# Two queue positions at a kernel's start, and where GpSimd's staging loads may stand

## The chip, the cores and the metric

The kernel runs on one core of one Trainium2 chip. The metric is the device time of one execution in microseconds. Smaller is better. A core has five engines that run their own queues of instructions in order: TensorE (PE in the profile, with its weight loads as PEld), VectorE (DVE), ScalarE (ACT), GpSimd (POOL) and SyncE (SP, which here only issues transfers). GpSimd and ScalarE can issue transfers too.

## The reference, cut to what matters

An encoder layer on two batches (prompt and sample, 1024 rows of 1024 channels each): RMS norm, one wide input projection, a Fourier branch, a Hyena branch with two long convolutions per channel block, gates, and an output projection. The Hyena filters come from a small network with two sine layers.

```python
xn = rmsnorm(x, g_pre)
p = xn @ w_in                                     # 8 sections of 1024 columns
fz = fft(fv, axes=(sequence, channel in group)).real
y_f = (fz * silu(fg)) @ w_fourier_out
h = sin(f1 * (z @ w1 + b1)); h = sin(f2 * (h @ w2 + b2)); h = h @ w3   # filters, then windowed
z = v
for n, gate in enumerate((x1, x2)):
    z = gate * long_conv(z, kf[:, n], hyena_d[n])
y_h = (z * silu(hg)) @ w_hyena_out
out = (g_f * y_f + g_h * y_h) @ w_out
return x + rmsnorm(out, g_post)
```

## The kernel before, in words

Three phases follow each other: `phase_fourier`, `phase_main`, `phase_blocks`. All matrices are split into a rounded high part and a rest (`split`, lines 168 to 174: ScalarE casts the high part, VectorE or GpSimd subtracts), so that a product is three matmuls (`mm3`).

**The start** (batch 0 in `phase_fourier`). `hidden(0)` computes the first sine layer of the filter network: two matmuls, then on VectorE the range reduction of `sin_of` (lines 255 to 270) for two halves, then a Sin on ScalarE for each half (line 270), then a store to DRAM on SP (line 299). `norm` (line 302) loads eight blocks of 128 rows, squares each on ScalarE with the sum beside it (line 319), and for every four blocks computes on VectorE the inverse root (`rstd`, 11 short dependent steps) and scales four identity blocks with it (`dg`, line 324). Those diagonal blocks are the right-hand sides of the transposing matmuls `tpx` in `xtile` (line 342), whose results ScalarE copies out as `xg` (line 343). From `xg` VectorE makes even and odd parts `eo`, split into `eh` and `el`. `weights` (line 359) loads a block `wfv` of the first weights into one of two buffers, adds and subtracts its halves on VectorE (`wer`, `wor`), casts on ScalarE (`we`, `wo`) and subtracts on VectorE. Six projections (`pfv`) run along with the eight column blocks k. The tables `seq` and `chan` are loaded by GpSimd after a one-column copy from `rs` (lines 528 to 532), so not before the inverse roots are there.

**Staging** (`staging`, lines 911 to 934). In the sample batch of `branches`, each convolution step draws twice from a generator of 25 steps. A piece (of 24: three operands q, four k, two halves) is two loads into a buffer `draw` on GpSimd's queue (line 926), eight subtractions and additions of 128x256 on GpSimd (`fold`), and a store to `d_t` (line 932), for the last operand a second store to `d_wo` (line 930). There are two `draw` buffers. The operands are read in `phase_blocks`. Operand 1 is made of `d_g[0][0]`, which the filter stage of `phase_main` writes, operand 2 of `d_sh[0]`, which the prompt batch's convolutions write, and operand 5 of `w_out`. GpSimd also subtracts the low parts `wl` of the input projection's weights (`inproj`, line 716) up to the end of the prompt batch, and multiplies its gates.

**What sets the order.** The Tile framework schedules each engine's queue ahead of time from its own timing of the whole program. `tc.issue_after(ins)` makes the instructions that a block creates on the engine of `ins` follow `ins` in that engine's queue; instructions on other engines get no edge. `self.spectrum` (line 799) is a load that SP issues, and the block at line 923 creates loads on GpSimd.

Of the kernel before, what the change touches and what calls it, by code (L numbers as in the profile page):

```python
# [161 lines left out]
class K:  # L162
# [92 lines left out]
    def sin_of(self, y, k, out, src_ps, f, b):  # L255

        nc = self.nc
        nc.vector.tensor_scalar(y, src_ps, b, f, op0=ADD, op1=MUL)
        magic = 12582912.0
        nc.vector.tensor_scalar(k, y, 1.0 / (2 * math.pi), magic, op0=MUL, op1=ADD)  # L260
        nc.vector.tensor_scalar(k, k, -magic, None, op0=ADD)
        c1 = 6.28125
        r = 2 * math.pi - c1
        c2 = float(_round12(np.array([r]))[0])
        c3 = r - c2
        for c in (c1, c2, c3):
            self.stt("dve", y, k, -c, y)
        pi = 3.1415925
        nc.vector.tensor_scalar(y, y, pi, -pi, op0=ALU.min, op1=ALU.max)
        nc.scalar.activation(out, y, AF.Sin)  # L270

    def hidden(self, layer, px, pf):

        nc, a = self.nc, self.a
        h = px.tile([P, L], F32, tag="eo", name=f"hd_{layer}", bufs=2)
        out = [h[:, 0:512], h[:, 512:1024]]
        z = px.tile([P, L], F32, tag="x", name="hd_z", bufs=3)
        if layer == 0:
            w = pf.tile([P, P], F32, tag="sst", name="hd_w", bufs=1)
            self.hfb = px.tile([P, 4], F32, name="hd_fb", bufs=1)  # L280
            nc.sync.dma_start(z[0:33], a["c_z"])
            nc.scalar.dma_start(w[0:33], a["filt_w1"])
            nc.scalar.dma_start(self.hfb, a["filt_fb"])
            w, z = w[0:33], z[0:33]
            y, k = [[pf.tile([P, 512], F32, tag=f"{t}p{n}", name=f"s{t}", bufs=1 + (t == "p")) for n in range(2)]
                    for t in "qp"]
        else:
            nc.sync.dma_start(z[64:128], self.d_h1[64:128])
            w = px.tile([P, P], F32, tag="xg", name="hd_w", bufs=2)
            nc.sync.dma_start(w[64:128], a["filt_w2"])  # L290
            w, z = w[64:128], z[64:128]
            y, k = [px.tile([P, L], F32, tag="x", name="s" + t, bufs=3) for t in "yk"]
            y, k = [[t[:, 0:512], t[:, 512:1024]] for t in (y, k)]
        for n in range(2):
            p = self.psum("mm", 4, "phd")
            nc.tensor.matmul(p, w, z[:, 512 * n:512 * n + 512], start=True, stop=True)
            self.sin_of(y[n], k[n], out[n], p, self.hfb[:, 2 * layer:2 * layer + 1],
                        self.hfb[:, 2 * layer + 1:2 * layer + 2])
        nc.sync.dma_start(self.d_h if layer else self.d_h1, h)


    def norm(self, b, px, pf):

        nc, a = self.nc, self.a
        ss = px.tile([P, 8], F32, tag="ss", name=f"ss{b}")
        self.rs = rs = px.tile([P, 8], F32, tag="rs", name=f"rs{b}")
        self.diag = dg = px.tile([P, 8, P], F32, tag="dg", name=f"dg{b}", bufs=1)
        self.xs = []  # L310
        for m in range(8):
            if b == 0 and m < 6:
                x = pf.tile([P, D], F32, tag=("fA", "fB", "ee0", "ee1", "oo0", "oo1")[m], name=f"x0_{m}", bufs=1)
            else:
                x = px.tile([P, D], F32, tag="x", name=f"x{b}_{m}", bufs=3)
            nc.sync.dma_start(x, a[f"x{b}"][m * P:(m + 1) * P, :])
            self.xs.append(x)
            sq = px.tile([P, D], F32, tag="xg", name="sq", bufs=2)
            nc.scalar.activation(sq, x, AF.Square, accum_out=ss[:, m:m + 1])
            if m % 4 == 3:  # L320
                q = slice(m - 3, m + 1)
                self.rstd(px, rs[:, q], ss[:, q], 4)
                for j in range(m - 3, m + 1):
                    nc.vector.tensor_scalar(dg[:, j], self.ident, rs[:, j:j + 1], None, op0=MUL)

    def xtile(self, b, k, px, fo):

# [157 lines left out]
    def phase_fourier(self):  # L485
        tc, nc, a = self.tc, self.nc, self.a
        with ExitStack() as es:
            px = es.enter_context(tc.tile_pool(name="px", bufs=1, reuse_waits="tile"))
            pw = es.enter_context(tc.tile_pool(name="fw", bufs=1, reuse_waits="tile"))
            pe = es.enter_context(tc.tile_pool(name="fe", bufs=1, reuse_waits="tile"))  # L490
            pc = es.enter_context(tc.tile_pool(name="fc", bufs=1, reuse_waits="tile"))
            pf = es.enter_context(tc.tile_pool(name="ff", bufs=1, reuse_waits="tile"))
            fo = {}
            fo["x5"] = pc.tile([P, 8, 36], F32R, name="x5")
            fo["x5t"] = pc.tile([P, 260], F32R, name="x5t")
            fo["xx"] = pc.tile([P, 34], F32R, name="xx")
            fo["px"] = pc.tile([P, 514], F32R, name="px")
            fo["ex"] = [pc.tile([P, 4, 34], F32R, name=f"ex{i}") for i in range(2)]
            fo["seq"] = pc.tile([P, 2, 8 * 258], F32R, name="seq")
            fo["alt"] = pc.tile([P, 2 * 86], F32R, name="alt")  # L500
            fo["chan"] = pc.tile([P, 2, 3 * P], F32R, name="chan")
            fo["chx"] = pc.tile([P, 2, 2, P], F32R, name="chx")
            for t in [fo[n] for n in ("x5", "x5t", "xx", "px")] + fo["ex"]:
                if len(t.shape) > 2:
                    t = t.rearrange("p a b -> p (a b)")
                nc.vector.tensor_scalar(t, self.ident[:, 0:1].to_broadcast(list(t.shape)), 0.0, None, op0=MUL)
            for b in range(NB):
                fo["eh"] = pe.tile([P, 8, 2, 2, 256], F32R, tag="eh", name="eh")
                fo["el"] = pe.tile([P, 8, 2, 2, 256], F32R, tag="el", name="el")
                if b == 0:  # L510
                    self.hidden(0, px, pf)
                with tc.issue_after(behind.ins) if b else ExitStack():
                    self.norm(b, px, pf)
                begun = {}
                if b == 0:
                    W = self.open_weights(pw)
                    for e, m in [(0, 0), (0, 1), (0, 2), (0, 3), (1, 0), (1, 1)]:
                        begun[e, m] = self.psum("X", 2, "pfv1") if e else self.psum("mm", 4, "pfv0")
                for k in range(8):
                    if b == 0:  # L520
                        self.weights(pw, W, 0, k, True)
                    self.xtile(b, k, px, fo)
                    for (e, m), p in begun.items():
                        self.pfv(p, e, m, k, W, fo)
                for half in ((0, 1), (1, 0))[b]:
                    if b + half == 0:
                        nc.sync.dma_start(self.vec, a["c_vec"])
                        for t in ("seq", "chan"):
                            nc.gpsimd.tensor_copy(fo[t][:, 0, 0:1], self.rs[:, 7:8])
                        nc.gpsimd.dma_start(fo["seq"], a["c_seq"])  # L530
                        nc.gpsimd.dma_start(fo["alt"], a["c_alt"])
                        nc.gpsimd.dma_start(fo["chan"], a["c_chan"])
                        nc.gpsimd.dma_start(fo["chx"].rearrange("p a b c -> p (a b c)"), a["c_chx"])
                    elif b + half != 2:
                        W = self.open_weights(pw)
                        for k in range(8):
                            self.weights(pw, W, half, k, False)
                        behind = self.rounded
                    self.fourier_half(b, half, W, fo, px, pf, begun)
                    begun = {}  # L540
                    if (b, half) == (1, 1):
                        self.hidden(1, px, pf)


    def butterfly(self, ws, xp, xm):
# [170 lines left out]
    def inproj(self, sec, mt, b=None):  # L716
# [3 lines left out]
        for q in range(2):  # L720
# [8 lines left out]
            else:  # L729
                r = self.wp.tile([P, 512], F32, tag="w", name="wr", bufs=2)  # L730
                nc.sync.dma_start(r, a["w_in"][sec, mt][:, s])
                self.split(*parts, r, "pool", "act")
                if kept:
                    for t, k in zip(parts, kept):
                        nc.gpsimd.dma_start(k[:, s], t.bitcast(F32))
# [175 lines left out]
    def staging(self):  # L911
# [3 lines left out]
        for q, k, half in [(q, k, h) for q in (1, 2, 5) for k in range(4) for h in range(2)] + [(0, 0, 0)]:  # L915
            r = None
            if q:
# [2 lines left out]
                    r = self.stage2.tile([P, 4, 256], F32, tag="draw2", name="draw", bufs=1)  # L920
                else:
                    r = self.cp.tile([P, 4, 256], F32, tag="draw", name="draw", bufs=1)
                with self.tc.issue_after(self.spectrum.ins):
                    for i in range(2):
                        src = {1: self.d_g[0][0], 2: self.d_sh[0]}[q][k + 4 * i] if q < 5 else a["w_out"][(k + 4 * i) * P:(k + 4 * i + 1) * P]
                        nc.gpsimd.dma_start(r[:, 2 * i:2 * i + 2], src.rearrange("p (n c) -> p n c", n=2)[:, :, s])
# [548 lines left out]
```

## Time and profile before

| | us |
|---|---|
| median of 3 runs (2438.82 to 2448.58) | 2444.28 |
| the profiled execution, its own time | 2439.01 |
| its span, first to last instruction | 2437.2 |
| TensorE busy in the span | 2366.3 |
| VectorE, ScalarE, GpSimd busy | 2034.0, 1126.2, 563.5 |
| TensorE busy of the first 40 us | 18.80 |
| TensorE busy of 400 to 800 us | 380.12 |
| TensorE busy of 1200 to 1500 us | 298.51 |

The profile is one execution. A row of its timeline gives start, duration, engine, source line, operation, output and inputs; a bracket at the end gives the idle time before the row and what ended it. A row of the list of waits gives who waited for whom, the total in us, how often, and the longest. A row of groups gives the busy time, the mean duration in ns, and the idle time before. SPq and POOLq are the transfer issues and queue events of those engines.

### The profile page before, as it was taken

The page shows a single profiled execution, that of the slowest core. Times are in us where ns is not written, and L with a number is a line of the kernel's source. Part 1 is how long each engine was busy: PE and PEld are TensorE (multiplying, and loading weights), DVE is VectorE, ACT ScalarE, POOL GpSimd, SP SyncE. Part 2 cuts the span into 40 slices and gives each one's busy share as a digit, 9 for nine tenths or more (in the row PEclk, how much of TensorE's full clock was granted, in tenths as well). Part 3 has the DMA queues.
Part 4 walks back from the last instruction along what each step waited for, and adds up shares of the span by engine and source line. Part 5 has one row for each costly group of instructions (what it writes and reads, how often), then busy time and mean ns, then how long its engine had stood idle before and what let it go on. Part 6 is the DMA issues. An engine that isn't in the chain of part 4 may idle for free.

```text
span 2437.2 us, 37123 instructions
## 1 busy us (share of the span) xinstructions
PE 2366.3 (97%) x13006; PEld 2053.1 (84%) x13006; DVE 2034.0 (83%) x3816; ACT 1126.2 (46%) x2088; POOL 563.5 (23%) x568
## 2 busy tenths in 40 slices
PE   6999999999999999999999999999999999999998
PEld 5988888887878888888888888888878888888786
DVE  7687788788888999999999999997667687778777
ACT  5545666665554333333332222333334365656543
POOL 1341322233343343434334400111200000101000
PEclk9999999999999999999999999999999999999999
DMA  7535644466566455555667644343646687978744
GB/s 272 181 133 203 226 158 156 160 190 186 189 202 211 152 182 177 168 161 174 223 199 265 209 143 137 130 153 128 213 143 219 214 304 249 279 263 227 227 156 155
DMA packets 246850, 470.26 MB, mean 193 GB/s; under 512 B 24758, under 2 KB 88471, under 8 KB 246280
## 3 DMA queue, kind: packets, MB, share of 16 engines
q1 hardware_dynamic: 220076, 380.53, 47.7%
q0 software_dynamic: 26400, 87.35, 10.8%
q8 instruction: 102, 1.67, 0.3%
q14 instruction: 84, 0.69, 0.1%
q10 hardware_dynamic: 188, 0.02, 0.0%
HBM read 300.04 MB, written 167.77 MB: 192 GB/s over the span
## 4 chain that ended last, share of the span: by engine, by line
PE 50%; DMA 1%; DVE 1%; issue 0%; ACT 0%; SPq 0%; DVEq 0%; ACTq 0%
PE pg L194 25%; PE pin L194 16%; PE pT L194 4%; PE pX L194 4%; DMA wh<-d_w 1%; PE tph L787 1%; DMA bl<-d_t 0%; DMA wraw<-d_m 0%; DVE bl L181 0%; DVE wraw L181 0%; DVE gt L181 0%; DVE o L181 0%; DVE o L177 0%; ACT bh L1034 0%; ACT pg L1142 0%
## 5 line engine op out<-in xcount | busy, mean ns | idle before, releaser
L194 PE MATMUL pin<-xh,wh 128*128 128x512 f32 x1472 | 577.9, 394 | 6.4 <-ACT wh L171 1.9
L194 PE MATMUL pin<-xh,wl 128*128 128x512 f32 x1472 | 576.9, 393 | 2.1 <-POOL wl L181 2.1
L194 PE MATMUL pin<-xl,wh 128*128 128x512 f32 x1472 | 578.2, 393 | 0.0
L181 POOL TENSOR_TENSOR wl<-wr,wh 128x512 fp32r<-128x512 f32 x136 | 243.5, 1790 | 885.0 <-ACT wh L171 657.4
L194 PEld LDWEIGHTS pin<-xh,wh 128*128 128x128 f32 x1472 | 277.9, 189 | 58.2 <-DMA wh<-d_w 2.7
L194 PEld LDWEIGHTS pin<-xh,wl 128*128 128x128 f32 x1472 | 278.4, 189 | 53.5 <-POOL wl L181 2.9
L194 PEld LDWEIGHTS pin<-xl,wh 128*128 128x128 f32 x1472 | 278.2, 189 | 50.9
L194 PE MATMUL pT<-cinv,yh 128*128 128x256 f32 x1024 | 192.2, 282 | 0.0
L194 PEld LDWEIGHTS pT<-cinv,yh 128*128 128x128 f32 x1024 | 165.1, 190 | 9.7
L181 DVE TENSOR_TENSOR t<-pX,k 128x1024 f32<-128x1024 f32 x128 | 155.4, 1214 | 8.7 <-PE pX L194 6.6
L194 PE MATMUL pX<-bh,cfwd 128*128 128x256 f32 x768 | 160.7, 287 | 0.2 <-ACT bh L171 0.2
L171 ACT CAST wh<-wr 128x512 fp32r<-128x512 f32 x136 | 83.8, 616 | 150.9 <-PE pin L194 107.0
L171 ACT CAST yh<-y 128x512 fp32r<-128x512 f32 x128 | 79.4, 621 | 160.3 <-DVE y L181 133.4
L194 PE MATMUL pT<-cinv,yl 128*128 128x256 f32 x512 | 144.9, 283 | 1.1 <-DVE yl L181 1.1
L171 ACT CAST bh<-b 128x512 fp32r<-128x512 f32 x144 | 88.7, 619 | 111.4 <-DVE b L181 71.8
L181 DVE TENSOR_TENSOR bl<-b,bh 128x512 fp32r<-128x512 f32 x144 | 115.1, 801 | 19.1 <-ACT bh L171 18.9
L194 PEld LDWEIGHTS pX<-bh,cfwd 128*128 128x128 f32 x768 | 125.7, 191 | 3.6 <-ACT bh L171 0.6
L194 PE MATMUL pX<-bl,cfwd 128*128 128x256 f32 x384 | 109.5, 285 | 0.0
L1231 POOL DMA_DIRECT2D d_m<-gt x32 | 27.5, 860 | 320.2 <-DVE gt L181 288.4
L194 PEld LDWEIGHTS pT<-cinv,yl 128*128 128x128 f32 x512 | 97.7, 191 | 3.5 <-DVE yl L181 1.6
L181 DVE TENSOR_TENSOR yl<-y,yh 128x512 fp32r<-128x512 f32 x128 | 94.2, 736 | 6.5 <-ACT yh L171 6.4
L181 DVE TENSOR_TENSOR y<-t 128x512 f32<-128x512 f32 x128 | 97.6, 763 | 0.8
(354 smaller groups left out, 5718.6 us busy)
## 6 DMA issues: line engine op xcount, KB each, us to landing
k<-d_k SPq DMA_DIRECT2D x128, 512.0 KB, 4.3
wr<-in_w_in SPq DMA_DIRECT2D x136, 256.0 KB, 3.2
d_g<-gt SPq DMA_DIRECT2D x92, 256.0 KB, 2.6
d_k<-kt SPq DMA_DIRECT2D x128, 128.0 KB, 2.2
d_k<-kt SPq DMA_DIRECT2D x64, 256.0 KB, 2.6
fz<-d_g SPq DMA_DIRECT2D x64, 256.0 KB, 5.2
d_t<-draw POOLq DMA_DIRECT2D x24, 512.0 KB, 5.1
d_w<-wh POOLq DMA_DIRECT2D x48, 256.0 KB, 4.0
```

The costliest lines, as they stand in the source:

```text
L171: self.rounded = nc.scalar.copy(h, src)
L181: return e.tensor_tensor(out, a, b, op=op)
L194: return self.nc.tensor.matmul(out, lhsT, rhs, start=start, stop=stop, skip_group_check=shared)
L787: nc.tensor.transpose(tp[:, q * P:(q + 1) * P], eo[:, e, q], self.ident)
L1231: at(t + 0.3, lambda: nc.gpsimd.dma_start(d_m[:, c], box[0], accum_op=ADD))
```

## The change

Three edits. First, `sin_of` no longer issues the Sin; `hidden` returns a function that does so and stores the result, and for the first layer it is called after `norm`, inside `issue_after` the last square. Second, the first weights' blocks are traced inside `issue_after` the last of the eight diagonal scalings, which acts on what `weights` does on VectorE. Third, the staging loads are held behind `self.pooled`, the last subtraction that `inproj` put on GpSimd, instead of `self.spectrum`.

```diff
@@ sin_of
         nc.vector.tensor_scalar(y, y, pi, -pi, op0=ALU.min, op1=ALU.max)
-        nc.scalar.activation(out, y, AF.Sin)
@@ hidden
-        nc.sync.dma_start(self.d_h if layer else self.d_h1, h)
+
+        def sines():
+            for n in range(2):
+                nc.scalar.activation(out[n], y[n], AF.Sin)
+            nc.sync.dma_start(self.d_h if layer else self.d_h1, h)
+        return sines
@@ norm
-            nc.scalar.activation(sq, x, AF.Square, accum_out=ss[:, m:m + 1])
+            self.squared = nc.scalar.activation(sq, x, AF.Square, accum_out=ss[:, m:m + 1])
...
-                    nc.vector.tensor_scalar(dg[:, j], self.ident, rs[:, j:j + 1], None, op0=MUL)
+                    self.scaled = nc.vector.tensor_scalar(dg[:, j], self.ident, rs[:, j:j + 1], None, op0=MUL)
@@ phase_fourier
                 if b == 0:
-                    self.hidden(0, px, pf)
+                    sines = self.hidden(0, px, pf)
                 with tc.issue_after(behind.ins) if b else ExitStack():
                     self.norm(b, px, pf)
+                if b == 0:
+                    with tc.issue_after(self.squared.ins):
+                        sines()
...
                     if b == 0:
-                        self.weights(pw, W, 0, k, True)
+                        with tc.issue_after(self.scaled.ins):
+                            self.weights(pw, W, 0, k, True)
...
-                        self.hidden(1, px, pf)
+                        self.hidden(1, px, pf)()
@@ inproj
                 self.split(*parts, r, "pool", "act")
+                self.pooled = self.left
@@ staging
-                with self.tc.issue_after(self.spectrum.ins):
+                with self.tc.issue_after(self.pooled.ins):
```

ScalarE's queue at the start before the change, from the fifth block's square to the first `xg` copy (`sq` is the output of a square and also the tile that a Sin reads):

```order
L319 ACTIVATE sq,ss_328<-x_4_364 128x1024
L270 ACT_TABLE_LOAD
L270 ACTIVATE hd_296<-sq 128x512
L319 ACTIVATE sq,ss_328<-x_5_368 128x1024
L270 ACTIVATE hd_296<-sq 128x512
L319 ACTIVATE sq,ss_328<-x_6_372 128x1024
L319 ACTIVATE sq,ss_328<-x_7_376 128x1024
L343 ACTIVATE xg_0_417<-tpx,gpre 128x512
```

The same stretch of ScalarE's queue with the change:

```order
L323 ACTIVATE sq,ss_325<-x_4_361 128x1024
L323 ACTIVATE sq,ss_325<-x_5_365 128x1024
L323 ACTIVATE sq,ss_325<-x_6_369 128x1024
L323 ACTIVATE sq,ss_325<-x_7_373 128x1024
L301 ACT_TABLE_LOAD
L301 ACTIVATE hd_296<-sq 128x512 x2
L347 ACTIVATE xg_0_417<-tpx,gpre 128x512
```

The table load and both Sins moved from between the squares to between the last square and the first copy.

VectorE's queue before, from the first four diagonal blocks into the second inverse root (`rs_m`, `rs_329`, `rs_t` are that root's steps):

```order
L324 TENSOR_SCALAR dg_330<-ident,rs_329 128x128 x4
L181 TENSOR_TENSOR wer<-wfv 128x260
L181 TENSOR_TENSOR wor<-wfv 128x256
L241 TENSOR_SCALAR rs_m<-ss_328 128x4
L181 TENSOR_TENSOR wer<-wfv 128x260
L181 TENSOR_TENSOR wor<-wfv 128x256
L242 TENSOR_SCALAR rs_329<-rs_m 128x4
L181 TENSOR_TENSOR we_398<-wer,we_397 128x260
L250 SCALAR_TENSOR_TENSOR rs_t<-rs_329 128x4
L181 TENSOR_TENSOR wo_400<-wor,wo_399 128x256
```

VectorE's queue with the change, from the last step of the second inverse root:

```order
L252 SCALAR_TENSOR_TENSOR rs_326<-rs_t,rs_326 128x4
L328 TENSOR_SCALAR dg_327<-ident,rs_326 128x128 x4
L181 TENSOR_TENSOR wer<-wfv 128x260
L181 TENSOR_TENSOR wor<-wfv 128x256
L181 TENSOR_TENSOR wer<-wfv 128x260
L181 TENSOR_TENSOR wor<-wfv 128x256
L181 TENSOR_TENSOR we_398<-wer,we_397 128x260
L181 TENSOR_TENSOR wo_400<-wor,wo_399 128x256
```

The eight operations on the weights of k = 0 and 1, which stood between the steps of the second root, now stand behind its diagonal blocks. On ScalarE the casts of the weights of k = 2 now stand ahead of the copies `xg_2` and those of k = 3 behind them; before, ahead of `xg_2` stood the casts of k = 4 and 5.

GpSimd's queue before, around the second piece of operand 1 (`d_g_0_1` and `d_g_0_5` are written in the filter stage):

```order
L926 DMA draw<-d_g_0_1_126 128x2x256 x2
L181 TENSOR_TENSOR wl<-wr,wh 128x512 x6
L926 DMA draw<-d_g_0_5_130 128x2x256 x2
L181 TENSOR_TENSOR wl<-wr,wh 128x512
L181 TENSOR_TENSOR draw<-draw 128x256 x8
L932 DMA d_t_241<-draw 128x4x256 x2
```

GpSimd's queue with the change, where the first pieces of operand 1 now stand, at the end of the prompt batch:

```order
L744 DMA d_w_7_1_236<-wl 128x512
L181 TENSOR_TENSOR wl<-wr,wh 128x512 x2
L935 DMA draw<-d_g_0_0_125 128x2x256
L935 DMA draw<-d_g_0_4_129 128x2x256
L935 DMA draw<-d_g_0_0_125 128x2x256
L935 DMA draw<-d_g_0_4_129 128x2x256
L181 TENSOR_TENSOR draw<-draw 128x256 x7
L941 DMA d_t_241<-draw 128x4x256
```

All 24 pieces now stand behind the last `wl` of the prompt batch; before, the eight of operand 1 stood in the filter stage and the first of operand 2 in the prompt batch's convolutions. On TensorE and VectorE the queues of the convolution stage hold the same instructions in another interleaving.

## Prediction

> **What bounds the kernel now.** First the page, for the busy shares, then the list of TensorE's waits, then stretches, then the timeline of the stretches in which TensorE idles.
>
> ```profile
> PE 2366.3 (97%) x13006; PEld 2053.1 (84%) x13006; DVE 2034.0 (83%) x3816; ACT 1126.2 (46%) x2088; POOL 563.5 (23%) x568
> PE tpx L194 <- DVE dg L324: 14.5, 2, 8.9
> 0.00:40.00 40.00, 18.80 (x94) 15.43 (x95) 27.35 (x86) 22.71 (x40) 4.38 (x17) 0.98 0.85 290
> 40.00:60.00 20.00, 20.00 (x166) 20.00 (x166) 18.04 (x40) 13.54 (x20) 3.52 (x6) 0.95 0.68 232
> 400.00:800.00 400.00, 380.12 (x2030) 325.40 (x2030) 336.06 (x735) 230.69 (x492) 139.90 (x134) 0.98 0.58 188
> ```
>
> TensorE bounds the kernel: of 2437.2 us of span it idles 70.9. Of these, 21.2 lie in the first 40 us, where the transposes wait 14.5 for the diagonals, and 19.9 in the 400 us that hold the filter stage. From 40 us on TensorE is full, so time that the start gains is kept. The change can only win out of these two patches and a few waits near 1130 us, and can only lose where TensorE is now full.
>
> **Edits 1 and 2, the start: the last square.** In the timeline of the start:
>
> ```profile
> 13.02 0.33 SPq L886 DMA_DIRECT2D th<-in_c_th  x1
> 13.08 1.06 ACT L319 ACTIVATE sq<-x 128x1024 f32<-128x1024 f32 x1 [0.67 <-DMA x<-in_x]
> 14.25 1.28 ACT L270 ACT_TABLE_LOAD   x1
> 14.28 0.33 SPq L886 DMA_DIRECT2D wsh<-in_w_short  x1
> 15.54 0.63 ACT L270 ACTIVATE hd<-sq 128x512 f32<-128x512 f32 x1
> 15.55 0.33 SPq L886 DMA_DIRECT2D bm<-in_b_merge  x1
> 16.08 1.04 ACT L319 ACTIVATE sq<-x 128x1024 f32<-128x1024 f32 x1
> 18.68 1.04 ACT L319 ACTIVATE sq<-x 128x1024 f32<-128x1024 f32 x1
> 19.84 0.17 DVE L241 TENSOR_SCALAR rs_m<-ss 128x4 f32<-128x4 f32 x1 [1.56 <-ACT sq L319]
> ```
>
> Table load and two Sins (1.28 + 2 x 0.63 = 2.5 us) stand before the last three squares. Without them the squares wait for their rows. SP's small issues are released one per landed block of x: the fifth square starts at 13.08, next to the issue at 13.02, so the sixth and seventh blocks landed near 14.3 and 15.6, and I take 16.9 for the eighth by the same spacing. The last square then runs from 16.9 to 17.95 instead of to 19.72: 1.8 us.
>
> **The second root and its diagonals.**
>
> ```profile
> 22.41 0.16 DVE L250 SCALAR_TENSOR_TENSOR rs_t<-rs 128x4 f32<-128x4 f32 x1
> 23.59 0.88 DVE L324 TENSOR_SCALAR dg<-ident,rs 128x128 f32<-128x128 f32 x4
> 23.93 7.04 PE L194 MATMUL tpx<-dg,x 128*128 128x128 f32 x40 [5.59 <-DVE dg L324]
> ```
>
> From the first step at 19.84 to the diagonals at 23.59 it takes 3.75 us, because eight operations on weights stand in between. The last six steps, free of them, take 23.59 - 22.41 = 1.18, 0.20 each, so 11 take 2.2: 1.55 us less. The diagonals come 1.8 + 1.55 = 3.3 us earlier, near 20.3.
>
> **What is late next.** The table load and two Sins (2.5 us) now stand between the last square (18.1 with its accumulator read) and the first xg copy, which comes at 20.7; TensorE needs the bank that this copy frees from about 21.0, so this costs some 0.4 us. The eight weight operations follow the diagonals (0.35 apart, 2.8 us, from 21.2) and are covered by the transposes (7.04). The real price is in the loads: a buffer of wfv is free only when its sums are done.
>
> ```profile
> 24.10 0.53 POOL L530 DMA_DIRECT2D seq<-in_c_seq  x1 [0.18 <-POOL chan L529]
> L363 SPq DMA_DIRECT2D wfv<-in_w_fv x2: 328/328/328, 18.3 to 20.7; - x2
> DMA to landing us min/median/max: 2.9/3.1/3.3
> ...
> L363 SPq DMA_DIRECT2D wfv<-in_w_fv x1: 328/328/328, 25.2 to 25.2; - x1
> DMA to landing us min/median/max: 10.2/10.2/10.2
> 35.41 0.43 DVE L181 TENSOR_TENSOR wer<-wfv 128x260 f32<-128x260 f32 x1 [1.78 <-DMA wfv<-in_w_fv]
> 37.96 1.27 ACT L343 ACTIVATE xg<-tpx,gpre 128x512 f32<-128x512 f32 x2
> 38.70 4.57 PE L194 MATMUL tpx<-dg,x 128*128 128x128 f32 x24 [3.10 <-ACT xg L343]
> ```
>
> The two weight blocks issued at 18.3 and 20.7 are those of k = 2 and 3; they land in about 3.1 us. The one issued at 25.2, of k = 4, is caught behind seq on the shared DMA engines: 10.2 us, until 35.4. ScalarE has the casts of k = 4 and 5 ahead of xg_2, so TensorE's transposes of k = 3 wait until 38.70. With the change seq is issued near 20.9, and now k = 2 and 3 are caught behind it: issued near 22.1 and 22.8 (sums done; the store of the sine layer, which SP issues ahead of them, is ready at 20.7), landing near 22.1 + 10.2 + 1 = 33.3 (the store's bytes share the engines) and 34.3. But only k = 2 stands ahead of xg_2, so the copies run at about 34.3 and the transposes at 35.0: 38.70 - 35.0 = 3.7 us. Bounds: a landing after 3.1 us would leave the limit to the 3.3 us of the diagonals plus up to 2.2 of the chain behind, 5.5; a landing at 35.5 leaves 1.5. k = 4 and 5 are issued after that without seq and land in about 3.1 us, before the projections ask. **First term: -3.7.**
>
> A rule of the Trainium skill ("ScalarE: Activation LUTs", What ACT_TABLE_LOAD costs) puts a drain of 1.38 us behind each table load of 1.28. The row at 14.25 ends at 15.53 and the Sin starts at 15.54, so the trace shows the load and no drain. By the page the first copy would come 1.4 us later and the term would be about -2.3, an estimate.
>
> **Edit 3, what leaves the prompt batch.** The old block named an instruction of SP, and the loads are GpSimd's, so they were not held and GpSimd waited for them with other work behind.
>
> ```profile
> L181 POOL TENSOR_TENSOR draw<-draw x32: 717/741/1190, 487.1 to 681.0; 128x256 f32<-128x256 f32 x32
> 545.54 1.44 POOL L926 DMA_DIRECT2D draw<-d_g  x2 [6.84 <-DMA d_g<-gt]
> 546.27 2.58 DVE L181 TENSOR_TENSOR bl<-b,bh 128x512 fp32r<-128x512 f32 x1
> L181 DVE TENSOR_TENSOR bl<-b,bh 128x512 fp32r<-128x512 f32 x10 | 6.8, 683 | 2.5 <-ACT bh L171 2.5
> 548.91 0.39 PE L194 MATMUL pXf<-bl,cfwd 128*128 128x256 f32 x1 [1.00 <-DVE bl L181]
> 558.84 0.36 PE L194 MATMUL pXf<-bh,cfwd 128*128 128x256 f32 x1 [2.09 <-DVE kt L177]
> 682.45 0.36 PE L194 MATMUL pXf<-bh,cfwd 128*128 128x256 f32 x1 [1.08 <-ACT dec L621]
> 1132.95 0.50 PE L194 MATMUL pin<-xh,wl 128*128 128x512 f32 x1 [1.27 <-POOL wl L181]
> 1137.31 0.71 PE L194 MATMUL pX<-b,cfw 128*128 128x128 f32 x4 [1.12 <-DVE b L181]
> ```
>
> The first row is operand 1's folds in the filter stage. At 546 VectorE's bl (0.68 in a stretch without staging, the group row) lasts 2.58 beside GpSimd's late issues and the wl behind them; TensorE waits 1.00 and then 2.09. After the last fold of 681 it waits 1.08, and near 1133 1.27 and 1.12, where the first piece of operand 2 stands ahead of a wl. Together 6.6 us stand close behind a piece. Upper bound: all the idle time of that stretch, (681 - 487)/400 x 19.9 = 9.7, and the last two waits, 12.0 in all. Lower bound: 0, if the next wait takes the place. Most of VectorE's other work stays where it is, so I take three quarters of 6.6: **-5.**
>
> "SBUF — State Buffer" of the Trainium skill (Who interferes with whom) says that a VectorE instruction with two SBUF inputs contends with a GpSimd instruction that reads SBUF, and infers that descriptor generation does not hold tensor_tensor. By that the 2.58 is the fault of the wl, which stays, and this term would be about -2.
>
> **Edit 3, what comes to the sample batch.** All 24 pieces now run one behind the other once the prompt batch's last wl is done. The pieces of operand 2 no longer wait for d_sh, since eight others stand ahead of them, and the results are read only in the last phase, so there is no deadline near.
>
> ```profile
> 1280.00:1376.00 96.00, 94.51 (x573) 84.15 (x573) 90.84 (x158) 26.41 (x46) 54.06 (x64) 1.00 0.77 259
> 1376.00:1570.00 194.00, 194.00 (x1166) 172.76 (x1165) 184.43 (x344) 57.72 (x97) 4.91 (x4) 1.00 0.43 139
> L181 DVE TENSOR_TENSOR y<-t 128x512 f32<-128x512 f32 x13 | 10.8, 834 | 0.1
> L181 DVE TENSOR_TENSOR y<-t 128x512 f32<-128x512 f32 x14 | 9.6, 682 | 0.0
> L930 POOL DMA_DIRECT2D d_wo<-draw x8: 757/757/777, 1287.2 to 1368.1; - x8
> L932 POOL DMA_DIRECT2D d_t<-draw x16: 757/770/775, 1119.2 to 1375.5; - x16
> ```
>
> The first stretch holds operand 5's eight pieces (the eight d_wo, 96/8 = 12 us each), the second almost none; y takes 834 ns beside the folds (row of 1270 to 1370) and 682 without (1380 to 1480). Over all, 158 operations in 90.84 us are 575 ns, 344 in 184.43 are 536: 39 ns times 158 is 6.2 us for eight pieces, 0.77 a piece. VectorE's slack without staging is (194 - 184.43)/194 = 4.9%. Before, 16 pieces in some 270 us (the d_t stores, and 12 us ahead of the first) cost 16 x 0.77 = 12.3 of 0.049 x 270 = 13.2 us of slack: just covered. Now 24 at 11 us each, as 16 have no second store, take 264 us and cost 18.5 against 12.9: 5.6 over, less for those 16. **Third term: +4**, from 0 (TensorE's run-ahead covers it) to the first rival's price.
>
> The new interleaving in the convolutions I cost at nothing, give or take 3 us: same instructions, and TensorE's idle time there is under 1% with the old one.
>
> **Sum.** -3.7 - 5 + 4 = -4.7. The profiled execution took 2439.0, so 2434.3 of its kind; the median, 2444.3, lies 5.3 above it: 2439.6, say 2439.5. About 0.5%, 12.2 us, is what a measurement of this kernel can tell from no change.
>
> **The rivals.**
> *VectorE becomes the bound in the sample batch.* If each piece costs VectorE what bl lost at 546, 2.58 - 0.68 = 1.9, then 24 x 1.9 - 12.9 = 32.7 us are lost, and with the gains of 8.7 the result is 24 us slower: 2468.3. It decides from (12.9 + 8.7)/24 = 0.90 us a piece. Against it: the measured 0.77 includes everything. For it: 0.77 is close, and the pieces now run without pauses. 7%.
> *The start gains nothing.* The loads of k = 2 and 3 land at 37 or later behind seq and the store; 2444.3 - 5 + 4 = 2443.3. For it: landing took 10.2 us, and now hits two blocks that it spared before. 20%.
> *Everything is covered.* TensorE's run-ahead hides VectorE's stretch, the start gains 5, and all 12.0 us of waits go: 2444.3 - 5 - 12.0 = 2427.3, over 0.5% faster. 12%.
> *The third edit does nothing.* The order shows the loads moved, so this has no chance of its own.
>
> **How the numbers follow.** Forecast 61%, rivals 7, 20 and 12. Faster by over 0.5%: the third rival, 0.12. Slower by over 0.5%: the first, 0.07. Within: 0.81. The range runs from just above the third rival's price, 2428, to 2449: the second rival's with a third term 5.7 us larger.
>
> **What would show it.** Right: rs_m near 18.1, dg near 20.3, one Sin pair behind the last square, the wait for xg_2 ending near 35 instead of 38.7; no draw row between 480 and 690 and bl near 0.7 there; all 24 d_t stores in some 264 us behind the last wl of the prompt batch, with VectorE at 98% or more. Wrong: the weights of k = 2 landing past 36; TensorE losing over 10 us in that stretch; new waits of pin for wh or wl.

## The result and the profile after

The changed kernel takes 2447.01 us (median of 22 runs, 2441.22 to 2451.18), the kernel before 2441.19 beside it (22 runs). The ratio is 1.0020, 95% interval 1.0013 to 1.0027: 4.9 us slower, 3.2 to 6.6. The time lies in the predicted range and within 0.5% of before; the sign is the other one: forecast was faster, measured is slower. In what follows, a difference in us is the ratio's distance from 1 times 2441 us.

The busy line of the changed kernel's page:

```profile
PE 2372.7 (97%) x13006; PEld 2057.0 (84%) x13006; DVE 2053.2 (84%) x3816; ACT 1124.8 (46%) x2088; POOL 554.5 (23%) x568
```

Its stretches (us, then busy time and count of TensorE, its weight loads, VectorE, ScalarE and GpSimd, granted clock, DMA share, GB/s):

```profile
0.00:40.00 40.00, 22.16 (x119) 18.59 (x120) 26.95 (x84) 24.19 (x41) 4.48 (x18) 1.00 0.81 290
40.00:60.00 20.00, 17.65 (x147) 17.04 (x146) 18.96 (x41) 12.06 (x20) 3.08 (x5) 1.00 0.71 236
400.00:800.00 400.00, 385.78 (x2064) 332.32 (x2063) 336.62 (x741) 232.81 (x496) 102.49 (x84) 0.98 0.52 171
1100.00:1400.00 300.00, 287.38 (x1667) 251.45 (x1666) 291.85 (x464) 87.38 (x143) 166.34 (x189) 0.98 0.69 237
```

The last stretch in the kernel before:

```profile
1100.00:1400.00 300.00, 295.16 (x1738) 260.28 (x1737) 283.57 (x487) 92.10 (x151) 119.83 (x131) 1.00 0.63 214
```

TensorE does the same 13006 matmuls, so the count in a stretch says about how far it got. The changed kernel does 25 matmuls more in the first 40 us and 19 fewer in the next 20; 34 more from 400 to 800; and 71 fewer from 1100 to 1400, where a matmul takes 295.16/1738 = 0.170 us: 12.1 us lost around the change of batches. Of these, 7.8 are idle time (287.38 busy for 295.16); the rest goes with a lower granted clock (0.98 for 1.00).

The start of the changed kernel, rows of the timeline of ScalarE, VectorE and TensorE (start, duration, engine, line, operation; in brackets the idle time before and what ended it):

```profile
17.01 1.06 ACT L323 ACTIVATE sq<-x 128x1024 f32<-128x1024 f32 x1
18.18 1.28 ACT L301 ACT_TABLE_LOAD   x1
18.19 0.17 DVE L241 TENSOR_SCALAR rs_m<-ss 128x4 f32<-128x4 f32 x1
19.47 1.15 ACT L301 ACTIVATE hd<-sq 128x512 f32<-128x512 f32 x2
20.37 0.88 DVE L328 TENSOR_SCALAR dg<-ident,rs 128x128 f32<-128x128 f32 x4
20.72 7.71 PE L194 MATMUL tpx<-dg,x 128*128 128x128 f32 x40 [1.06 <-DVE dg L328]
32.03 0.43 DVE L181 TENSOR_TENSOR wer<-wfv 128x260 f32<-128x260 f32 x1 [2.33 <-DMA wfv<-in_w_fv]
33.98 0.75 PE L194 MATMUL pfv<-we,el 128*128 128x260 f32 x4 [1.90 <-DVE el L181]
35.28 1.27 ACT L347 ACTIVATE xg<-tpx,gpre 128x512 f32<-128x512 f32 x2 [2.05 <-DMA d_x<-xg]
36.02 3.23 PE L194 MATMUL tpx<-dg,x 128*128 128x128 f32 x24 [1.05 <-ACT xg L347]
46.80 2.05 PE L194 MATMUL tpx<-dg,x 128*128 128x128 f32 x16 [1.17 <-ACT xg L347]
55.68 0.76 PE L194 MATMUL pfv<-we,el 128*128 128x260 f32 x4 [0.77 <-DVE el L181]
```

Everything up to the diagonals comes as forecast. The transposes of k = 3 begin at 36.02 in place of 38.70, and then TensorE waits at 46.80 and 55.68, where before it was full.

The staging's stores in the changed kernel (durations in ns, first and last start):

```profile
L941 POOL DMA_DIRECT2D d_t<-draw x24: 772/776/786, 1153.2 to 1387.5; - x24
```

The change of batches in its timeline, rows of GpSimd, VectorE and TensorE:

```profile
1147.88 5.33 POOL L181 TENSOR_TENSOR draw<-draw 128x256 f32<-128x256 f32 x5
1152.54 2.42 DVE L181 TENSOR_TENSOR b<-xt 128x256 f32<-128x256 f32 x3
1155.29 2.45 DVE L181 TENSOR_TENSOR y<-t 128x512 f32<-128x512 f32 x1
1155.67 0.39 PE L194 MATMUL pX<-bh,cfwd 128*128 128x256 f32 x1 [1.01 <-ACT bh L171]
1155.91 1.27 POOL L181 TENSOR_TENSOR x<-x,sg 128x512 f32<-128x512 f32 x1
1158.50 0.50 PE L194 MATMUL pT<-cinv,yh 128*128 128x256 f32 x2 [2.44 <-ACT yh L171]
1189.99 0.50 PE L194 MATMUL pin<-xh,wh 128*128 128x512 f32 x1 [3.32 <-DMA wh<-d_w]
```

and two stretches of it of 5 us:

```profile
1155.00:1160.00 5.00, 1.60 (x6) 1.03 (x7) 5.00 (x6) 2.79 (x5) 2.05 (x2) 1.00 1.03 416
1160.00:1165.00 5.00, 5.00 (x17) 3.85 (x16) 5.00 (x10) 1.94 (x3) 4.12 (x5) 0.66 1.03 415
```

All 24 pieces are stored from 1153 to 1388. The first folds (the additions and subtractions of a staging piece) stand exactly where the second batch's x arrives: VectorE is busy for all of these 10 us, the DMA share is 1.03, and TensorE, which before waited 0.38 from 1150 to 1200, waits 1.01, 2.44 and then 3.32. After the first two waits its clock is granted at 0.66. The change of batches has no room to begin with: in the kernel before, VectorE is busy for 49.80 of the 50 us from 1150 to 1200.

Two slow operations of VectorE stand next to GpSimd's work. Three b take 2.42 us beside the folds (0.82 in the run without folds). One y takes 2.45 (0.68 without staging), but the last fold near it ended at 1154.81; what stands beside this y is the issue of a staging store and then the gate multiplication (`x<-x,sg`), which is not staging.

### The profile page after: what moved, and what is told of

It is laid out like the page before. It is cut to its first block, busy times and chain, and to the rows that moved or that the text cites. A ratio compares the mean times of both kernels' runs of the same rounds, so it can differ in the third digit from the quotient of the medians.

```text
span 2443.9 us, 37108 instructions
## 1 busy us (share of the span) xinstructions
PE 2372.7 (97%) x13006; PEld 2057.0 (84%) x13006; DVE 2053.2 (84%) x3816; ACT 1124.8 (46%) x2088; POOL 554.5 (23%) x568
## 5 line engine op out<-in xcount | busy, mean ns | idle before, releaser
L181 POOL TENSOR_TENSOR wl<-wr,wh 128x512 fp32r<-128x512 f32 x136 | 227.4, 1673 | 964.7 <-ACT wh L171 935.5
L181 POOL TENSOR_TENSOR draw<-draw 128x256 f32<-128x256 f32 x96 | 93.9, 989 | 41.3 <-DMA draw<-d_g 14.5
```

The costliest lines, as they stand in the source:

```text
L181: return e.tensor_tensor(out, a, b, op=op)
```

## The experiments

The theory on going in (A): the staging collides with the second batch's x at the change of batches. Rivals: the transfers alone (B), the order that the scheduler gave the convolutions after another start (C, later called O), and the sheer amount of folds (D). The scheduler orders the queues by a simulated time line, so an edit at the start can reorder the convolutions 1000 us later. In the traces such orders differ between some 740 and 1800 us.

**One part alone: the first two edits.**

```diff
-                with self.tc.issue_after(self.pooled.ins):
+                with self.tc.issue_after(self.spectrum.ins):
```

> The first two edits alone, staging loads as before. Theory A (the loss is the staging's collision with the second batch's xl subtractions near 1150 to 1200 us; the start keeps only a little): 1 to 2 us faster than before, TensorE's losses of 1150 to 1200 us gone, the wait of pn still near 437.5. Prediction's first term: 3.7 us faster. Rival C (the other start lets the scheduler order the convolutions otherwise, and that loses the time): 4 to 7 us slower than before, as with all three edits.

Measured: ratio 1.0016 (1.0005 to 1.0027), 3.9 us slower. The first edits alone lose nearly all that the change loses, with the staging where it was. Theory A does not explain that; C's number, 4 to 7, is missed by only 0.1.

**One part alone: the third edit,** on the kernel before.

> The third edit alone, start as before. Theory A: 5 to 8 us slower than before, the filter stage some 8 us shorter and the stretch of 1100 to 1300 us some 15 longer, with waits and a lower granted clock near 1155 to 1195 as with all three edits. Rival C (the start's order): no slower than before, or up to 5 us faster as the prediction's second term alone has it.

Measured: 0.9996 (0.9986 to 1.0006), 1.0 us faster, give or take 2.4. A does not explain the net loss; the prediction's sum for this edit, -5 + 4, came true. Its profile shows both terms:

```profile
300.00:800.00 500.00, 485.06 (x2610) 418.15 (x2609) 420.41 (x952) 300.63 (x646) 127.05 (x97) 0.99 0.52 167
1100.00:1400.00 300.00, 287.96 (x1705) 252.72 (x1704) 293.93 (x471) 90.83 (x148) 180.36 (x188) 1.00 0.71 238
```

From 300 to 800 us it does 2610 matmuls for 2568 before, which at 0.187 us each is 7.8 us gained, and from 1100 to 1400 it does 1705 for 1738, 5.6 us lost. So the collision that A names is there, but the filter stage gains more than it costs.

**The staging held until the second batch's x is split.**

```diff
+                if q == 1 and k == 0:
+                    nc.gpsimd.tensor_copy(r[:, 0, 0:1], self.xl[7][:, 0:1].bitcast(F32))
                 with self.tc.issue_after(self.pooled.ins):
```

> All edits, but the first two pieces wait, by a one-element copy on GpSimd, for the second batch's last xl subtraction. Theory A (place): the waits of 1150 to 1195 us go, the filter stage's gain stays: 6 to 10 us faster than before, some 2432 to 2435. Rival D (amount: 24 pieces in some 250 us slow VectorE wherever they stand): within 2 us of the time with all three edits, 4 to 6 us slower than before, the waits moved to 1180 to 1450.

Measured: 0.9985 (0.9968 to 1.0002), inconclusive between no change and 8 us, and so between A and D. In its profile 1100 to 1200 has 568 matmuls (487 with all edits), but 1200 to 1400 has 1081 (1182): there the loss moved along with the pieces. That profile is of the longest of its twelve runs, 2448.53 us for a median of 2440.85, so it may show more loss than is usual. That both place and density count is suggested by it, not shown.

**Two pieces to a convolution,** each behind its group's spectrum tile.

```diff
+                nc.gpsimd.tensor_copy(r[:, 0, 0:1], self.ktile[:, 0, 0:1])
                 with self.tc.issue_after(self.pooled.ins):
...
+            self.ktile = kt
             if stage and g in (0, 1):
```

> All edits, and each piece waits, by a one-element copy on GpSimd, for the spectrum tile of its own convolution group, so that the 24 pieces stand two to a convolution over some 440 us in place of 234, the first after the second batch's first spectrum load. Theory A (place): as with the pieces held behind the last xl subtraction, 6 to 10 us faster than before. Rival D (amount and density): clearly faster than holding the first two alone, by 4 us or more, as VectorE's slack grows to twice as much for the same folds.

Measured: 1.0129 (1.0110 to 1.0148), 31 us slower: neither theory. Up to 1400 it did 1776 matmuls from 1100 on (1738 before), then broke off: 445 from 1500 to 1600, against 600. I put this down to its last pieces, which stood ahead of the last weights' subtractions on GpSimd: of TensorE's waits from 1500 to 1660 us, 19.2 are for these subtractions (`wl`) and 9.8 for a load of `wh`. So I tried three a convolution.

```diff
-            if stage and g in (0, 1):
+            if stage and g != 2:
```

> All three edits, and each piece of the staging waits, by a one-element copy on GpSimd, for the spectrum tile of its own group, three pieces to a convolution in place of two, so that the last stands near 1490 and not at 1612 us. Theory T (two to a convolution was slow only because its last pieces stood ahead of the last weights' subtractions on GpSimd): 8 to 14 us faster than before, the lead of the filter stage kept past 1300 us. Rival (a dense staging costs as much wherever it stands): 0 to 6 us slower than before.

Measured: 1.0119 (1.0104 to 1.0134), 29 us slower. My reason was not the whole of it: TensorE's waits for the subtractions are gone, but nearly all of the loss is still there. The largest of the waits of SP's queue from 1360 to 1560 us and of TensorE's from 1280 to 1600 (who waits for whom: total, times, longest):

```profile
SPq L808 <- POOL draw L933: 96.7, 11, 14.8
...
PE pin L194 <- DMA wh<-d_w: 22.5, 4, 8.8
```

and one of them in the timeline of SP's queue and of TensorE (two spectrum loads take 12.46 us on the queue):

```profile
1369.84 12.46 SPq L808 DMA_DIRECT2D k<-d_k  x2
1382.41 0.38 SPq L736 DMA_DIRECT2D wh<-d_w  x1
1388.57 0.79 PE L194 MATMUL pin<-xh,wh 128*128 128x512 f32 x1 [5.09 <-DMA wh<-d_w]
```

The copy that paced the pieces reads a spectrum buffer, so this buffer is free only when GpSimd has come to it. The next spectrum load waits for that on SP's queue, up to 14.8 us, and the weights' loads stand behind it. The wait was my own. In the run with two pieces a convolution the spectrum loads wait for GpSimd as well, 32.1 us from 1500 to 1650.

**Three pieces to a convolution, behind a mark** that holds no buffer of the path.

```diff
+                nc.gpsimd.tensor_copy(r[:, 0, 0:1], self.mark[:, self.marks - 1:self.marks])
                 with self.tc.issue_after(self.pooled.ins):
...
             self.split(yh, yl, Y, "dve", "act")
+            if stage and g in (0, 2, 1) and self.marks < 25:
+                nc.scalar.copy(self.mark[:, self.marks:self.marks + 1], yh[:, 0, 0, 0:1].bitcast(F32))
+                self.marks += 1
+                next(stage, None)
```

> All three edits, three pieces to a convolution, each piece waiting for a one-element mark that ScalarE writes after the cast of its group, so that no spectrum buffer is held for GpSimd and no load behind it on the load queue. Theory T' (the pieces paced by the spectrum tile lost their time in spectrum loads that waited for GpSimd's copy, with the weights' loads behind them): 5 to 12 us faster than before, no wait of a spectrum load for GpSimd. Rival D (a piece costs what it costs wherever it stands in the convolutions): within 4 us of before.

Measured: 0.9948 (0.9936 to 0.9959), 12.7 us faster than before: it beats both kernels. Among SP's waits from 1140 to 1640 us there is none of a spectrum load for GpSimd any more. The stores of its pieces:

```profile
L944 POOL DMA_DIRECT2D d_t<-draw x24: 769/774/792, 1239.2 to 1531.0; - x24
```

Its stretch of 1100 to 1400:

```profile
1100.00:1400.00 300.00, 296.88 (x1743) 260.70 (x1742) 287.03 (x485) 94.50 (x166) 111.43 (x128) 1.00 0.60 198
```

TensorE's waits in it from 1100 to 1640 us (total, times, longest):

```profile
PE pin L194 <- DMA wh<-d_w: 1.4, 1, 1.4
PE pX L194 <- DVE t L181: 0.6, 1, 0.6
PE pT L194 <- ACT yh L171: 0.6, 1, 0.6
PE pin L194 <- DMA wl<-d_w: 0.2, 1, 0.2
```

The same list for all three edits as they were:

```profile
PE pT L194 <- ACT yh L171: 5.5, 4, 2.4
PE pin L194 <- DMA wh<-d_w: 3.3, 1, 3.3
PE pX L194 <- DVE t L181: 1.9, 1, 1.9
PE pX L194 <- ACT bh L171: 1.0, 1, 1.0
...
```

2.8 us of waits in place of some 12.4, for the same 24 pieces, begun 86 us later and spread over 292 us in place of 234. Up to 1140 us its queues are those of the changed kernel; behind that the scheduler gave it an order of its own.

**Without the folds.**

```diff
-                self.fold("pool", [r_[:, j] for j in range(4)])
```

> All three edits without the staging's folds (the 96 additions and subtractions on GpSimd are left out; its loads and stores stay). Theory A (folds and VectorE's operations slow each other near the change of batches): 4 to 9 us faster than before, waits for VectorE and ScalarE of 1150 to 1260 us gone. Rival B (the staging's transfers): within 3 us of the time with all three edits, the waits for wh and wl still there.

A piece has four of these operations, 96 in all (the eight named at the start of this document are those of two pieces). Without them the staged operands are wrong, so the run only says what the folds cost.

Measured: 0.9973 (0.9961 to 0.9985), 6.6 us faster than before, so some 11.5 faster than with the folds. From 1100 to 1400 it does 1748 matmuls for 1667, and VectorE's y takes 0.69 us on average there, 0.81 with the folds. That is A's side: where they stand so densely, the folds slow VectorE, and the transfers, all still there, do not cost such a time. Two things limit it. Behind some 1150 us this kernel has an order of its own, and by what follows an order alone can be worth 6 of the 11.5. And folds are not all that slows VectorE: at 1160.22 one of its operations (bl, 0.69 elsewhere) takes 2.50 us beside two gate multiplications of GpSimd, with the staging's folds left out.

**The order alone.** The first two edits with every queue of the convolutions held, by edges of issue order, as the kernel before has it; and the kernel before with the order that the first two edits get. `follow` goes through a table of instruction positions, engine by engine, and adds an edge from each instruction to the one ahead of it.

```diff
+        first = len(tc.nc.cur_bb.bb.instructions)
         k.open_x(ctx)
         k.phase_main()
+        follow(tc, list(tc.nc.cur_bb.bb.instructions)[first:])
```

> The first two edits, and from the filter stage to the end of the convolutions every engine's queue held, by issue-order edges alone, in the order that the kernel before has there; staging as before. Theory O (what the first two edits cost is the other order that the scheduler gave the convolutions): 1 to 2 us faster than before, what the start keeps. Rival S (the moved sines and sums themselves cost the time): 4 to 5 us slower than before, as the two edits alone were.

Measured: 0.9994 (0.9984 to 1.0004), 1.5 us faster, as O had it, where the same edits with their own order were 3.9 slower.

The edges add nothing of their own: in the traces every queue of this kernel is, from 83 us on, that of the kernel before, instruction for instruction and with the same kinds of semaphore waits. The same holds for the other held kernels and those whose order they take.

> The kernel before with none of the three edits, and the same stretch held in the order that the first two edits alone have there. Theory O: 4 to 7 us slower than before, with nothing changed at the start and no staging moved. Rival S: within 2 us of before.

Measured: 1.0000 (0.9991 to 1.0009): as S had it. The new order under the old start costs nothing that could be measured. But its profile, too, has 1710 matmuls from 1100 to 1400, 28 fewer than before, where the first two edits have 29 fewer. From 83 us on it is the same program as the first two edits in their own order, and the intervals of the two (0.9991 to 1.0009 and 1.0005 to 1.0027) just overlap. Whether the old start makes the order free is open.

**All three edits in the order of the third alone.**

> All three edits, and from the filter stage to the end of the convolutions every engine's queue held in the order that the third edit alone has there. Theory O (the first two edits cost time through the order that the scheduler gave, not by themselves): 1 to 4 us faster than before, the first two edits worth some 1.5 us on top of the third's 1.0; so some 5 to 8 us faster than all three edits in their own order. Rival S: 4 to 6 us slower than before, as all three edits are.

Measured: 0.9995 (0.9981 to 1.0008), 1.2 us faster than before: O. The three edits are the same, and in the traces the queues of the two kernels are equal up to 735 us and again from 1780 us on; only the order between differs, and 6 us with it.

**The first edit alone, in its own order, and in that of the kernel before.**

> The first edit alone; its convolutions get a third order, unlike that of the kernel before and unlike that of the first two edits together. The start itself can bring at most what the two edits do, 1.5 us. Theory O: the time is that of the order, anywhere from 5 us slower to 5 us faster than before. Rival S: 0 to 2 us slower than before, a part of the two edits' 3.9.

Measured: 1.0020 (1.0009 to 1.0031), 4.9 us slower; more than S allows.

> The first edit alone, and from the filter stage to the end of the convolutions every engine's queue held in the order of the kernel before. Theory O: within 2 us of before, 1100 to 1400 us within 10 matmuls of before. Rival S: 3 to 7 us slower than before, as the first edit was in its own order (4.9).

Measured: 1.0001 (0.9991 to 1.0012), 0.2 us slower: O. Its stretch of 1100 to 1400 has 1731 matmuls.

**The second edit alone,** which gets the same order as the first two.

> The second edit alone; the scheduler gives its convolutions the same order as to the first two edits together. Theory O (the order costs the time): 2 to 5 us slower than before, 1100 to 1400 us some 25 matmuls short of before. Rival S (the first edit, the moved sines, costs the time): within 2 us of before, or faster.

Measured: 1.0011 (1.0001 to 1.0022), 2.7 us slower, so nearer to O; its one profile, though, shows 1735 matmuls from 1100 to 1400, not 25 fewer. In the trace its queues are those of the first two edits but for a few instructions of ScalarE in the first 20 us.

| edits | order of the convolutions | ratio to before | 1100 to 1400 us, matmuls |
|---|---|---|---|
| none | that of before | 1 | 1738 |
| 1 and 2 | that of before | 0.9994 | 1735 |
| 1 | that of before | 1.0001 | 1731 |
| 1 and 2 | their own | 1.0016 | 1709 |
| none | that of 1 and 2 | 1.0000 | 1710 |
| 2 | its own, that of 1 and 2 | 1.0011 | 1735 |
| 1 | its own | 1.0020 | 1722 |
| 1, 2 and 3 | that of 3 alone | 0.9995 | 1720 |
| 1, 2 and 3 | their own | 1.0020 | 1667 |

In this table every kernel with an edited start is slower than before in its own order, and none is when its order is held. The counts, each from one execution, do not rank the times: 1720 and 1710 stand beside 0.9995 and 1.0000. The two kernels of such a pair mostly ran on different chips, each with the kernel before beside it; on two of the chips a kernel in its own order was slower (1.0020 and 1.0011) and a held one was not (0.9995 and 1.0001), so the chip is an unlikely cause.

What the other order does at the change of batches is seen in the subtractions that split the second batch's x. With the first two edits in the old order:

```profile
1160.87 1.23 DVE L181 TENSOR_TENSOR xl<-xl,xh 128x1024 fp32r<-128x1024 f32 x1
1163.19 1.23 DVE L181 TENSOR_TENSOR xl<-xl,xh 128x1024 fp32r<-128x1024 f32 x1
1167.28 1.24 DVE L181 TENSOR_TENSOR xl<-xl,xh 128x1024 fp32r<-128x1024 f32 x1
...
1176.02 2.35 DVE L181 TENSOR_TENSOR xl<-xl,xh 128x1024 fp32r<-128x1024 f32 x2
```

and in their own:

```profile
1165.01 3.20 DVE L181 TENSOR_TENSOR xl<-xl,xh 128x1024 fp32r<-128x1024 f32 x2
...
1175.65 2.35 DVE L181 TENSOR_TENSOR xl<-xl,xh 128x1024 fp32r<-128x1024 f32 x2
1179.72 2.35 DVE L181 TENSOR_TENSOR xl<-xl,xh 128x1024 fp32r<-128x1024 f32 x2
```

In the old order the eight stand apart but for one pair, with the convolution's operations between them; in the other there are three pairs, and with all three edits two. The pairs alone do not cost the time: the kernel before in the new order has three of them and measured 1.0000, and the marked kernel has three and is the fastest. Which place of the order costs TensorE its time is not shown; the two orders differ in many places.

**The marked staging without the first two edits.**

> The third edit alone with the pieces paced by ScalarE's marks, three to a convolution, the start as before. If the pacing makes the gain: 9 to 14 us faster than before, as with all three edits (12.5). If the first two edits had a part in it: 5 us or more short of that.

Measured: 0.9956 (0.9942 to 0.9970), 10.7 us faster than before. The pacing makes the gain; the two edits have at most a small part in it. No run holds the order of the marked kernels. They gain 12.7 and 10.7 us with two different orders, more than the 6 us between two orders above, so an order alone is an unlikely cause, but it is not excluded.

## Why the prediction was wrong

**Its failed step: "The new interleaving in the convolutions I cost at nothing, give or take 3 us".** The same three edits are 1.2 us faster than before in one order and 4.9 slower in the one they got: 6.1 us. The first two edits show it without any staging moved (3.9 slower against 1.5 faster, 5.4) and so does the first alone (4.9 against 0.2). I looked at what moved near the edits and took TensorE's idle time under 1% in the old order as a sign that any order would do. It was a sign of that order. What stays open: under the old start the order of the first two edits cost 0.0 (give or take 2.2), so no price can be put on the order by itself, and which of its places decides was not isolated.

**First term, -3.7.** Up to the diagonals right: rs_m 18.19 (18.1), dg 20.37 (20.3), the first Sin at 19.47 right behind the table load's end at 19.46, so again no drain such as the Trainium skill ("ScalarE: Activation LUTs", What ACT_TABLE_LOAD costs) puts there. The weights of k = 2 landed at 32.03 (33.3); the copies came at 35.28 (34.3), as they waited for the store of the tile that they fill (2.05); the transposes at 36.02 (35.0), 2.7 us earlier. The mis-sized piece is "from 40 us on TensorE is full, so time that the start gains is kept": it was full behind a late start. In the changed kernel the next copies and sums of that stage are late (1.17 at 46.80, 0.77 at 55.68), and in the first 60 us it is 6 matmuls ahead, not 25. With the order held the two edits are worth 1.5 us (between 3.9 gained and 1.0 lost), and beside the third edit 0.2 (1.2 against 1.0).

**Second term, -5.** Right in place, too small in size: the filter stage gains 7.8 us with the third edit alone. There TensorE's waits from 480 to 690 us sum to 3.6 in place of 9.2, and those from 1105 to 1145, 3.0 before, are gone, so the mechanism is the one forecast.

**Third term, +4.** About right: 5.6 us from 1100 to 1400 with the third edit alone. That the folds cost VectorE its slack fits the run without them; but the loss is not spread over 264 us. With the third edit alone 26 of the 33 missing matmuls are missing from 1100 to 1200 (526 for 552), at the change of batches, where VectorE was full before. Second and third term together were forecast at -1 and measured at -1.0, give or take 2.4. That is partly luck: both are larger than forecast, and the errors cancel.

**The rivals.** "The start gains nothing" (2443.3) is nearest in time, but its mechanism did not occur: it needed the loads of k = 2 at 37 or later, and they landed at 32.03. "VectorE becomes the bound" decided from 0.90 us a piece on the average, and no average was needed: most of the loss stands where the first pieces meet the second batch's x. No rival said that the scheduler would give the convolutions another order and that this would cost.

## What to carry to other kernels

Where a scheduler orders the queues, an edit is two changes: what it does where it stands, and the order that everything behind it gets; before an effect under 1% is put down to the edit, hold the old order with issue-order edges and time that too. Background work on a shared engine can be paced by the loop that it hides behind, and begun after the transitions where the bound engine's feeders have no slack; here that gained 12.7 us. The mark that paces it should hold no buffer of the path: with a pacing read of a spectrum tile and the same three pieces a convolution the kernel was 29 us slower than before.

## What the runs showed of the hardware

A wait of TensorE can cost more than its length. TensorE in the changed kernel, after one wait of 1.93 us, and after a later one of 2.25:

```profile
1173.46 0.36 PE L194 MATMUL pX<-bh,cfwd 128*128 128x256 f32 x1 [1.93 <-DVE t L181]
...
1176.33 0.63 PE L194 MATMUL pin<-xh,wh 128*128 128x512 f32 x1
1176.76 0.59 PE L194 MATMUL pin<-xl,wh 128*128 128x512 f32 x1
1177.18 0.40 PE L194 MATMUL pin<-xh,wl 128*128 128x512 f32 x1
1177.42 0.39 PE L194 MATMUL pin<-xh,wh 128*128 128x512 f32 x1
1177.64 0.39 PE L194 MATMUL pin<-xh,wl 128*128 128x512 f32 x1
...
1257.44 0.51 PE L194 MATMUL pT<-cinv,yh 128*128 128x256 f32 x2 [2.25 <-ACT yh L171]
```

From 1173.8 to 1177.2 the clock is granted at 0.50: the pin matmuls stand 0.43 us apart, where 0.23 is usual. That is half the speed for 3.4 us, 1.7 us lost on top of the 1.93. After the wait of 3.32 at 1189.99 it is the same from 1190.80 to 1194.17. The wait of 2.25 that ended at 1257.44 has no such cost: the clock is granted at 1.00 from 1257 to 1267. The kernel before has a wait of 2.09 that ended at 558.84, also with 1.00 behind it. So in these traces the length of a wait alone does not decide. The Trainium skill ("TensorE: Matmul & The Clock Gate", Why this matters for your kernels) asks for no idle gap over some 3 us between bursts of matmuls; here half speed followed a gap of 1.93, so a shorter gap than that page of the Trainium skill names can cost as well.

Over whole runs the granted clock, averaged over each kernel's runs, was 0.9944 before and 0.9915 with all three edits. If all of the time scaled with it, the difference of 0.0029 would be 7.1 of 2440 us, an estimate. Time and clock go together within a kernel, too: of the twelve runs with the staging held behind the x subtractions, the shortest took 2424.07 us at 0.998 and the longest 2448.53 at 0.991. Which is the cause is not shown, as waits come first and the lower clock behind them. And the clock is not the whole of it: the first two edits alone lose their 3.9 us at an unchanged 0.9941, and the marked kernel is 12.7 us faster at 0.9937.
